# Seven products with four sums per side in the output projection and the feed-forward, the first normalisation on ScalarE

## The chip, the cores and the metric

The kernel runs on one core of a Trainium2 chip. The metric is the device time of one execution in microseconds (us). Times of several runs are given as their median; beside them stands one execution that the hardware profiler recorded, whose trace the profile is drawn from. The engines are TensorE (PE; its weight loads are listed apart as PEld), VectorE (DVE), ScalarE (ACT), GpSimd (POOL) and SyncE (SP), which here issues the DMAs.

## The reference, cut to what matters

One layer of a decoder block, 512 positions by 1024 channels, in float32:

```
p   = x @ W_in + b_in                       # split into u, v, q, k, v', r, low-rank gate, g_A, g_B
y_A = spatial gating unit(u, v)             # 128-position chunks, 8 groups
y_B = gated linear attention(q, k, v', ...) # 4 heads, RMSNorm, times silu(r)
m   = sigmoid(g_A) * y_A + sigmoid(g_B) * y_B
h   = LayerNorm(alpha * x + m @ W_out)              # W_out 1024 x 1024
out = LayerNorm(alpha * h + relu(h @ W_1)^2 @ W_2)  # W_1 1024 x 4096, W_2 4096 x 1024
```

The change touches the last two lines: the output projection with the first normalisation, and the feed-forward.

## The kernel before, in words

**Precision.** Each matmul operand is split (line 89 on ScalarE, line 90 on VectorE) into a high part, a cast to a shorter float format (fp32r), and a low part, the rest. A product is three matmuls: high by high, high by low, low by high.

**Weights.** All weights come in chunks of 128 x 1024 numbers, in the order that `_stream` lists. `load_to` issues the DMAs into a small ring, `sum_to` (line 124) forms sums or differences of chunks on VectorE where a product needs them, `split_to` splits a chunk into the next of seven pairs of buffers (wh, wl). A split therefore waits until TensorE has done with the chunk seven places back. Matmuls, and from line 588 on the instructions of VectorE, ScalarE and GpSimd too, run in the order in which the code emits them; DMAs on SP are placed by the compiler.

**Stages.** After the input projection, the gating unit and the attention (which are interleaved through slots, `at` and `pump`), `branch` handles two channel blocks of 128 at a time: two jobs for r, two for the gate B, each of 24 matmuls, and adds the result into AT_ (a view of bufA, channels on partitions). Each finished block is split into mh, ml, the operand of the output projection.

**Output projection.** Two calls of `row_unit` (columns 0 to 511, then 512 to 1023), each over four blocks of 128 rows, with 24 matmuls of 512 columns per block (line 213): 192 matmuls. `out_take` adds alpha * x on VectorE (line 869), takes statistics (870), and in the second call `ln_apply` normalises with scale g1 and shift b1 along the rows: two passes of 1024 on VectorE (640, 646), the power for 1/sqrt on GpSimd (171) between them.

**Turning.** The feed-forward needs h with channels on partitions. `turn_h` transposes a block of rows on TensorE (851) in two halves into the two PSUM banks of ps_a and splits each into hh, hl, which are the buffers of xh, xl. Rows 0 and 1 are turned during the second `row_unit`, rows 2 and 3 behind the first and third group of the feed-forward's first block: that block is run in two parts, positions 0 to 255, then 256 to 511.

**Feed-forward.** `col_group` (691) makes a hidden block of 128 channels in 24 matmuls; relu and square follow on ScalarE (915, 916). The second product, W_2, is done for three quarters of the hidden channels in pairs of blocks by seven block products instead of eight (`seven_products`, 986): operands are sums of blocks (`operand`, 912), each result is added to one of seven accumulators in SBUF (`keep`, 959 to 963), and `together` (997, 999) combines these at the end. One product alternates with one hidden block. The last quarter of W_2 is done plainly, row block by row block (1077), in column pieces of 512 and 512, for the last row block 512, 384 and 128; behind each piece VectorE adds and takes statistics (1078, 1079), and then normalises and stores the rows.

PSUM has eight banks: four single ones (ps_m), one pair (ps_s), and two single ones (ps_a).

Of the kernel before, what the change touches and what calls it, by code (L numbers as in the profile page):

```python
# [36 lines left out]
LANES = {0: RAW_BUFS, 1: 2}  # L37
PAIRS = 3
ORDER = (2, 6, 3, 7, 4, 1, 5)
LEVELS = (32, 8, 2)  # L40
ALS_AT = (0, 4, 48, 24, 12, 40, 56, 2)
# [5 lines left out]
def hybrid_block(  # L47
# [13 lines left out]
    ln1_b: bass.AP,  # L61
    ln2_g: bass.AP,
# [35 lines left out]
    raws, chunks, kept = {}, {}, {}  # L98
    lanes, ring = {0: rpool}, {lane: [] for lane in LANES}
    state = {"load": 0, "sum": 0, "split": 0}  # L100

    def load_to(n):
        while state["load"] < min(n, NCHUNK):
            i = state["load"]
            kind, lane, key, news = STREAM[i]
            if news is not None:
                ends = ring[lane]
                if len(ends) >= LANES[lane] and ends[-LANES[lane]] >= state["split"]:
                    break
                raw = lanes[lane].tile([P, 1024], F32, name=f"raw{i}", tag="raw")  # L110
                nc.sync.dma_start(raw, w_all[news])
                kept.setdefault(key, []).append(raw)
                users = [j for j in range(i + 1, NCHUNK) if STREAM[j][2] == key]
                users = [j for n_, j in enumerate(users) if all(STREAM[x][3] is None for x in users[:n_])]
                ends.append(max([i] + (users if key else [])))
            raws[i] = kept[key][-1:] if kind == "one" else kept[key][-2:]
            state["load"] = i + 1

    def sum_to(n):
        while state["sum"] < min(n, state["load"]):  # L120
            i = state["sum"]
            raw, *other = raws[i]
            if other:
                nc.vector.tensor_tensor(raw, raw, other[0], op=ALU.add if STREAM[i][0] == "sum" else ALU.subtract)  # L124
            state["sum"] = i + 1

    def split_to(n):
        n += n > ASIDE
        while state["split"] < min(n, NCHUNK):
# [8 lines left out]
            raw = raws[i][0]  # L138
# [4 lines left out]
        load_to(n + sum(LANES.values()) if 1 in lanes else n + RAW_BUFS)  # L143
# [106 lines left out]
    for i in range(4):  # L250
        raws[i] = [None]
# [31 lines left out]
    als_ = gt.tile([P, 1536], F32R, name="als", tag="qt", bufs=QT_BUFS)  # L283
    nc.vector.memset(als_.bitcast(F32), 0.0)
    als = []
    for k, o in enumerate(ALS_AT):
        als.append(als_[:, 192 * k + o : 192 * k + o + P])
        a4 = als[k].rearrange("p (r m) -> p r m", r=4)
        split(a4[:, 0, 0:RANK], a4[:, 3, 0:RANK], wal[:, k, :])
        nc.scalar.copy(a4[:, 1:3, 0:RANK], a4[:, 0:1, 0:RANK].bitcast(F32).broadcast_to([P, 2, RANK]))  # L290
# [32 lines left out]
    def low_rank():  # L323
        pa = ps_a.tile([P, 512], F32, name="pa", tag="aux")
        for k in range(KT):
            for i, xx in enumerate((xh, xl)):
                nc.tensor.matmul(
                    pa, als[k], xx[:, k, :], start=(k == 0 and i == 0), stop=(k == KT - 1 and i == 1)
# [465 lines left out]

    def r_take(e, t1):
# [25 lines left out]
    def branch(e0):  # L821
        t1 = {e: temp(f"t1_{e}", "brow") for e in (e0, e0 + 1)}
        for e in t1:
            col_job(f"r{e}", r_take(e, t1[e]))
        for e in t1:
            col_job(f"gb{e}", gb_take(e, t1[e]))
            if e0:
                split(mh[:, e, :], ml[:, e, :], AT_[:, e, :])

    branch(0)  # L830
# [6 lines left out]
    lnp.tile([P, 32], F32, name="pad_n")  # L837
    first_ln = ExitStack()
    ln1p = pool(first_ln, "ln1p", side="right")
    g1 = row_bcast(ln1p, ln1_g, D, "g1")  # L840
    b1 = row_bcast(ln1p, ln1_b, D, "b1")
    mstack = ExitStack()
    mpool = pool(mstack, "mpool", side="left")
    mh = mpool.tile([P, KT, T], F32R, name="mh")
    ml = mpool.tile([P, KT, T], F32R, name="ml")

    def turn(src, t, half, dh, dl):

        pt = ps_a.tile([P, 4, P], F32, name="pturn", tag="aux")
# [46 lines left out]

# [322 lines left out]
```

## Time and profile before

| | before |
|---|---|
| runs shown: median (lowest to highest) of 3 | 758.2 us (758.01 to 758.51) |
| the profiled execution | 757.96 us, span 756.2 us |
| granted TensorE clock, mean | 0.997 |

The page gives per engine the busy time, its share of the span and the instructions, then the span in 40 slices. The chain that ended last is followed back from the last instruction, and its shares say which engine the time hangs on. Groups of instructions by line show count, mean duration and what ended the idle time before them. A row of the timeline has start, duration, engine, line, operation, output and inputs, shapes, and a count where like instructions stand together. A row of the windows has for each stretch its length, the busy time of PE, PEld, DVE, ACT and POOL with the instructions in brackets, the granted clock, and the DMAs' share and rate. Matmuls are pipelined, so what one costs is read from start to start, not from its duration.

### The profile page before, as it was taken

How to read it: one execution, taken by the hardware profiler on the slowest of the kernel's cores; microseconds unless marked ns; L12 is line 12 of the kernel's file. 1: busy time of each engine (PE TensorE's matmuls, PEld its weight loads, DVE VectorE, ACT ScalarE, POOL GpSimd, SP SyncE). 2: the span in 40 equal slices, each digit the busy share in tenths (PEclk: the TensorE clock that was granted, in tenths of full speed). 3: DMA queues.
4: the chain of work that ended last, by engine and by line, in shares of the span. 5: the costliest groups of instructions: out<-in, count | busy, mean ns of one | idle time of the engine just before them, and what ended most of it. 6: DMA issues, size and time to landing. Idle time of an engine off the chain costs nothing.

```text
span 756.2 us, 8829 instructions
## 1 busy us (share of the span) xinstructions
PE 747.2 (99%) x3498; PEld 626.8 (83%) x3498; DVE 492.8 (65%) x618; ACT 349.5 (46%) x472; POOL 29.8 (4%) x60
## 2 busy tenths in 40 slices
PE   9999999999999999999999999999999999999996
PEld 7878888888888888888888988888888888888885
DVE  8478876676575554435458544874677667777995
ACT  7475744363254735444222544454644444445300
POOL 1000000000000102000002000000000000000011
PEclk9999999999999999999999999999999999999998
DMA  8623422222142131432341423444234333534111
GB/s 341 208 73 125 137 77 80 84 84 84 36 141 75 56 126 56 144 107 84 98 158 33 171 62 107 139 140 140 86 137 141 137 112 112 164 114 166 58 56 55
DMA packets 25465, 85.15 MB, mean 113 GB/s; under 512 B 3088, under 2 KB 3344, under 8 KB 25424
## 3 DMA queue, kind: packets, MB, share of 16 engines
q1 hardware_dynamic: 25280, 84.33, 32.4%
q8 instruction: 27, 0.44, 0.2%
q10 hardware_dynamic: 144, 0.26, 0.1%
q14 instruction: 14, 0.11, 0.1%
HBM read 82.48 MB, written 2.10 MB: 112 GB/s over the span
## 4 chain that ended last, share of the span: by engine, by line
PE 96%; issue 1%; DVE 1%; DMA 0%; POOL 0%; DVEq 0%; POOLq 0%
PE f L691 22%; PE ps L213 17%; PE m L986 15%; PE f L1077 6%; PE gb L691 6%; PE r L691 6%; PE ga L691 6%; PE u L691 6%; PE qk L691 3%; PE first L272 3%; PE sc L519 2%; PE pm L744 1%; PE po L553 1%; PE po L557 1%; PE po L555 1%
## 5 line engine op out<-in xcount | busy, mean ns | idle before, releaser
L90 DVE TENSOR_TENSOR wl<-raw,wh 128x1024 fp32r<-128x1024 f32 x141 | 171.2, 1222 | 99.2 <-ACT wh L89 97.7
L89 ACT CAST wh<-raw 128x1024 fp32r<-128x1024 f32 x141 | 145.7, 1044 | 51.1 <-PE ps L213 23.7
L691 PE MATMUL f<-xh,wh 128*128 128x512 f32 (+1 forms) x288 | 105.4, 366 | 0.0
L691 PE MATMUL f<-xl,wh 128*128 128x512 f32 (+1 forms) x288 | 105.3, 365 | 0.0
L691 PE MATMUL f<-xh,wl 128*128 128x512 f32 (+1 forms) x288 | 105.2, 365 | 0.0
L986 PE MATMUL m<-wh,oh 128*128 128x512 f32 x168 | 65.4, 389 | 0.0
L986 PE MATMUL m<-wl,oh 128*128 128x512 f32 x168 | 65.4, 389 | 0.0
L986 PE MATMUL m<-wh,ol 128*128 128x512 f32 x168 | 65.4, 389 | 0.0
L691 PEld LDWEIGHTS f<-xh,wl 128*128 128x128 f32 x288 | 54.3, 189 | 8.8
L691 PEld LDWEIGHTS f<-xh,wh 128*128 128x128 f32 x288 | 54.3, 189 | 8.7
L691 PEld LDWEIGHTS f<-xl,wh 128*128 128x128 f32 x288 | 54.3, 189 | 8.6
L213 PE MATMUL ps<-wh,xh 128*128 128x512 f32 x128 | 50.4, 394 | 0.0
L213 PE MATMUL ps<-wh,xl 128*128 128x512 f32 x128 | 49.8, 389 | 0.0
L213 PE MATMUL ps<-wl,xh 128*128 128x512 f32 x128 | 49.8, 389 | 0.0
L915 ACT ACTIVATE F<-f 128x512 f32<-128x512 f32 (+1 forms) x28 | 15.0, 536 | 70.7 <-PE f L691 70.7
L124 DVE TENSOR_TENSOR raw<-raw,raw 128x1024 f32<-128x1024 f32 x30 | 36.6, 1221 | 9.1 <-DMA raw<-in_w_all 9.1
L986 PEld LDWEIGHTS m<-wh,ol 128*128 128x128 f32 x168 | 31.5, 188 | 6.6
L986 PEld LDWEIGHTS m<-wh,oh 128*128 128x128 f32 x168 | 31.5, 188 | 6.6
L986 PEld LDWEIGHTS m<-wl,oh 128*128 128x128 f32 x168 | 31.5, 188 | 6.5
L89 ACT CAST oh<-d 128x1024 fp32r<-128x1024 f32 x15 | 15.7, 1049 | 36.4 <-DVE d L912 36.4
L90 DVE TENSOR_TENSOR ol<-d,oh 128x1024 fp32r<-128x1024 f32 x15 | 18.4, 1225 | 16.7 <-ACT oh L89 16.7
L213 PEld LDWEIGHTS ps<-wh,xl 128*128 128x128 f32 x128 | 24.0, 188 | 5.1
(231 smaller groups left out, 1477.1 us busy)
## 6 DMA issues: line engine op xcount, KB each, us to landing
raw<-in_w_all SPq DMA_DIRECT2D x136, 512.0 KB, 3.3
bufB<-in_head SPq DMA_DIRECT2D x4, 512.0 KB, 7.9
xr<-in_x SPq DMA_DIRECT2D x8, 256.0 KB, 3.6
out<-bufA SPq DMA_DIRECT2D x8, 256.0 KB, 2.0
bufA<-in_head SPq DMA_DIRECT2D x3, 512.0 KB, 5.3
brow<-in_b_in SPq DMA_DIRECT2D x4, 256.0 KB, 6.4
g<-in_ln_g SPq DMA_DIRECT2D x2, 512.0 KB, 4.0
b<-in_ln_b SPq DMA_DIRECT2D x2, 512.0 KB, 4.9
```

Source lines behind the costliest of these rows:

```text
L89: nc.scalar.copy(hi, src)
L90: nc.vector.tensor_tensor(lo, src, hi.bitcast(F32), op=ALU.subtract)
L124: nc.vector.tensor_tensor(raw, raw, other[0], op=ALU.add if STREAM[i][0] == "sum" else ALU.subtract)
L213: nc.tensor.matmul(ps, s_, m_, start=(k == 0 and i == 0), stop=(k == KT - 1 and i == 2))
L272: nc.tensor.matmul(first[e], s_, m_[:, k, :], start=(k == 0 and i == 0), stop=(k == KT - 1 and i == 2))
L519: nc.tensor.matmul(sc[:, c, 0:192], pr.kt[:, jc * P : (jc + 1) * P], pr.qt[:, jc, :], start=True, stop=True)
L553: nc.tensor.matmul(po, pr.AT[:, j, c, :], vs, start=True, stop=(c == 0))
L555: nc.tensor.matmul(po, pr.QI[:, j, c * P : (c + 1) * P], pr.S[j], start=False, stop=True)
L691: nc.tensor.matmul(ps, s_, m_, start=(k == 0 and i == 0), stop=(k == KT - 1 and i == 2))
L915: nc.scalar.activation(dst, ps, AF.Relu)
L986: nc.tensor.matmul(ps, s_, m_, start=(k == 0 and i == 0), stop=(k == 3 and i == 2))
L1077: nc.tensor.matmul(ps, s_, m_, start=(f == 0 and i == 0), stop=(f == 7 and i == 2))
```

## The change

The seven block products are done by another scheme, with a sum or difference in only four of seven operands on each side, and now in the output projection too. With A the left operand (positions by channels) and B the weights in 2 x 2 blocks:

```
product 1: A11 B11        2: A12 B21            5: S1 T1   S1 = A21+A22, T1 = B12-B11
product 6: S2 T2  S2 = S1-A11, T2 = B22-T1      3: S4 B22  S4 = A12-S2
product 7: S3 T3  S3 = A11-A21, T3 = B22-B12    4: A22 T4  T4 = B21-T2
x = 1, then +6, +7, +4 in one pair of PSUM banks (ps_s); v = 5, then +3 in ps_a
C11 = x(1) + 2;  C12 = x(1,6) + v(5,3);  C22 = v(5) + x(1,6,7);  C21 = x(1,6,7,4)
```

The order is 1, 2, 5, 6, 3, 7, 4. VectorE reads each bank after the product and adds it into bufA (projection) or bufB (feed-forward). The separate accumulators, the copies and `together` go. Products 7 and 4 follow each other on the same pair of banks; in the feed-forward a hidden block stands between any two products, in the projection none. The sums of the weights stay in SBUF (tiles "held", tags A and B), the ring of loads has three buffers, and W_out is laid out in quarters like W_2; two of its quarters are loaded twice.

The operands of the projection (seven blocks of 4 x 256 instead of the plain 8 x 512) are formed behind the branch jobs, whose channel blocks are paired anew. The first normalisation becomes one activation per row block on ScalarE without scale and shift; these are applied to channels in PSUM when the rows are turned, four pieces on ScalarE, four on VectorE, and for the kept rows by a multiplication and an addition on VectorE behind the jobs of the second hidden block. Rows 2 and 3 are turned behind the first and second group of the feed-forward. The operand of the low-rank gate is formed in fewer, larger instructions, in a buffer of the weights' ring. The last row block has pieces of 512, 256 and 256.

```diff
-ORDER = (2, 6, 3, 7, 4, 1, 5)
+ORDER = (1, 2, 5, 6, 3, 7, 4)
+PAIRED = ((0, 1), (4, 5), (2, 6), (3, 7))
...
+    def product_of(name, m, ops, take):
+        hi, lo = ops
+        u0 = take_chunks(2)
+        banks, begins = accumulators(m, name)
+        for t, ps in enumerate(banks):
+            tsl = slice(t * P, (t + 1) * P)
+            for k in range(4):
...
+                    nc.tensor.matmul(
+                        ps,
+                        s_,
+                        m_,
+                        start=(begins and k == 0 and i == 0),
...
+                if t and k % 2:
+                    split_to(u0 + k // 2 + 1 + W_BUFS)
+            take(m, t, ps)
...
+    def as_it_is(k, m, n=1):
...
+        split(mh[:, MADE[m] : MADE[m] + n, k, :], ml[:, MADE[m] : MADE[m] + n, k, :], src)
+
+    def summed(k):
...
+        nc.vector.tensor_tensor(s1, a(2, 1), a(2, 2), op=ALU.add)
+        for o, x_, y_ in ((s2, s1, a(1, 1)), (s4, a(1, 2), s2), (s3, a(1, 1), a(2, 1))):
+            nc.vector.tensor_tensor(o, x_, y_, op=ALU.subtract)
+        for i in range(2):
+            split(mh[:, 2 * i : 2 * i + 2, k, :], ml[:, 2 * i : 2 * i + 2, k, :], d[i])
...
+    branch(PAIRED[3], {3: [lambda: as_it_is(3, 1)], 7: [lambda: as_it_is(3, 2), *all_of(3)[1:]]})
...
+    def normalise(t):
+        row = bufA[:, t, :]
+        nc.scalar.activation(row, row, AF.Identity, bias=rs1[t][:, 1:2], scale=rs1[t][:, 0:1])
 
     def turn_h(t):
+
         for half in range(2):
-            turn(bufA[:, t, :], t, half, hh, hl)
-
-    row_unit(mh, ml, out_take(0))
-    at(S_O + 5, lambda: turn_h(0))
-    at(S_O + 6, lambda: turn_h(1))
-    row_unit(mh, ml, out_take(1))
+            pt = ps_a.tile([P, 4, P], F32, name="pturn", tag="aux")
+            for i in range(4):
+                e = half * 4 + i
+                nc.tensor.transpose(pt[:, i, :], bufA[:, t, e * P : (e + 1) * P], ident)
+            for i in range(4):
+                e = half * 4 + i
+                g_, b_ = ln1c[:, e : e + 1], ln1c[:, 8 + e : 9 + e]
+                if half:
+                    nc.vector.tensor_scalar(pt[:, i, :], pt[:, i, :], g_, b_, op0=ALU.mult, op1=ALU.add)
+                else:
+                    nc.scalar.activation(pt[:, i, :], pt[:, i, :], AF.Identity, bias=b_, scale=g_)
+            ks, tsl = slice(half * 4, half * 4 + 4), slice(t * P, (t + 1) * P)
+            split(hh[:, ks, tsl], hl[:, ks, tsl], pt)
+
+    def project_take(m, t, ps):
+        i, j = GOES[m]
+        dst, tt = quarter(bufA, i, j)[:, t, :], 2 * i + t
+        if m in NEW:
...
+            nc.vector.scalar_tensor_tensor(dst, xr, ALPHA, ps, op0=ALU.mult, op1=ALU.add)
+        else:
+            nc.vector.tensor_add(dst, dst, ps)
+        if m in (2, 3, 7, 4):
+            stats(tt, j)
+        if m in (3, 4):
+            rest_of_stats(tt)
+        if m == 7:
+            normalise(t)
+            if t:
+                turn_h(0)
+        if m == 4 and t == 0:
+            turn_h(1)
+        if m == 4 and t == 1:
+            normalise(2)
+
+    for m in ORDER:
+        product_of(f"o{m}", m, (mh[:, MADE[m]], ml[:, MADE[m]]), project_take)
+    normalise(3)
...
-            elif e in (0, 2):
-                turn_h(2 + e // 2)
-    for job in block(take_raw(F, 1)):
+            elif e in (0, 1):
+                turn_h(2 + e)
...
+    for t, job in enumerate(block(take_raw(F, 1))):
         job()
+        nc.vector.tensor_mul(bufA[:, t, :], bufA[:, t, :], g1)
+        nc.vector.tensor_add(bufA[:, t, :], bufA[:, t, :], b1)
...
-        pieces = ((0, 512), (512, 512)) if t < NT - 1 else ((0, 512), (512, 384), (896, 128))
+        pieces = ((0, 512), (512, 512)) if t < NT - 1 else ((0, 512), (512, 256), (768, 256))
```

More of the change, by code (lines that the diff above doesn't have):

```diff
@@ L104, in load_to @@
             i = state["load"]
[L105 to L108, printed above, removed]
+            c, own, *_ = STREAM[i]
+            if c is not None and own is None:
+                if len(ring) >= RAW_BUFS and ring[-RAW_BUFS] >= state["split"]:
                     break
[L110 to L116, printed above, removed]
+                kept[i] = rpool.tile([P, 1024], F32, name=f"raw{i}", tag="raw")
+                ring.append(i)
+            elif c is not None:
+                if "pool" not in held or held_to.get(own, -1) >= state["split"]:
+                    break
+                kept[i] = held[own] = held["pool"].tile([P, 1024], F32, name=f"raw{i}", tag=own)
+                held_to[own] = max(j for j in range(i, min(i + 40, NCHUNK)) if STREAM[j][3] == STREAM[i][3] and own in STREAM[j][2:])
+            if c is not None:
+                nc.sync.dma_start(kept[i], w_all[c])
             state["load"] = i + 1
@@ L121, in sum_to @@
             i = state["sum"]
-            raw, *other = raws[i]
-            if other:
-                nc.vector.tensor_tensor(raw, raw, other[0], op=ALU.add if STREAM[i][0] == "sum" else ALU.subtract)
+            _, own, dst, _, less = STREAM[i]
+            if dst is not None:
+                raw = held[dst]
+                if less:
+                    x_, y_ = (held[a] if a else kept[i] for a in less)
+                    nc.vector.tensor_tensor(raw, x_, y_, op=ALU.subtract)
+                kept[i] = raw
             state["sum"] = i + 1
@@ L843, in hybrid_block @@
     mpool = pool(mstack, "mpool", side="left")
[L844 to L849, printed above, removed]
-        for i in range(4):
-            nc.tensor.transpose(pt[:, i, :], src[:, (half * 4 + i) * P : (half * 4 + i + 1) * P], ident)
-        ks, tsl = slice(half * 4, half * 4 + 4), slice(t * P, (t + 1) * P)
-        split(dh[:, ks, tsl], dl[:, ks, tsl], pt)
@@ L855, in hybrid_block @@
[L855 to L876 removed]
+    mh = mpool.tile([P, 7, 4, 256], F32R, name="mh")
@@ L1079, in hybrid_block @@
             nc.vector.bn_stats(st2[t][:, pi, :], z[:, sl])
-            for part in later.get((t, pi), ()):
-                together(*part)
         mv = lnp.tile([P, 2], F32, name=f"mv_l2{t}", tag="mv", bufs=4)
@@ L1118, in _stream @@
     n = 15 * 4
-    out = [("one", 0, None, None)] * 4 + [("one", 0, None, c) for c in range(n)]
+    out = [(None, None, None, None, None)] * 4 + [(c, None, None, None, None) for c in range(n - 8)]
     f1 = n
@@ L1142, in _stream @@
             out += take(1 + (i == 0)) + product
-    out += [("one", 0, None, f2 + 8 * PAIRS + c) for c in range(8 * (DF // 1024 - PAIRS))]
+    out += [(f2 + 8 * PAIRS + c, None, None, None, None) for c in range(8 * (DF // 1024 - PAIRS))]
     return out
```

235 lines of the change are left out of this document (105 added, 130 removed).

## The prediction

> **What bounds the kernel now.** I read the page first: the share of each engine, then the chain that ended last.
>
> ```profile
> span 756.2 us, 8829 instructions
> ...
> PE 747.2 (99%) x3498; PEld 626.8 (83%) x3498; DVE 492.8 (65%) x618; ACT 349.5 (46%) x472; POOL 29.8 (4%) x60
> ...
> PE 96%; issue 1%; DVE 1%; DMA 0%; POOL 0%; DVEq 0%; POOLq 0%
> ```
>
> TensorE is the chain. To see what one matmul is worth I took the chain in order of time, where matmuls of one kind stand merged, and the windows view for the output projection.
>
> ```profile
> 367.46 32.64 PE ps L213 x144
> ...
> 423.57 47.06 PE f L691 x264
> 470.64 5.44 PE m L986 x24
> ```
>
> ```profile
> 367.46:412.60 45.14, 45.14 (x209) 37.53 (x208) 28.68 (x39) 11.78 (x14) 4.56 (x3) 1.00 0.28 92
> ```
>
> 24 matmuls of 512 columns advance the clock by 5.44 us, 0.2267 us each, although the groups show about 0.39 us for one: they overlap. The window begins at 367.46, where the last branch job (gb7) ends; I count from there below ("at 0"). PE is busy in all 45.14 us, VectorE in 28.68. So what PE issues less is gained in full, as long as VectorE, which has 16 us to spare there, can take what the change gives it.
>
> The third view is PE's timeline at the seam to the feed-forward, the only place there where PE waits.
>
> ```profile
> 412.61 0.28 PE L691 MATMUL f<-xh,wh 128*128 128x256 f32 x1
> ...
> 415.48 1.04 PE L851 MATMUL pturn<-ident,bufA 128*128 128x128 f32 x8
> 416.27 0.36 PE L691 MATMUL f<-xh,wh 128*128 128x256 f32 x1
> ...
> 421.99 0.28 PE L691 MATMUL f<-xh,wl 128*128 128x256 f32 x1
> 422.32 1.25 PE L851 MATMUL pturn<-ident,bufA 128*128 128x128 f32 x8
> 423.33 0.36 PE L691 MATMUL f<-xh,wh 128*128 128x256 f32 x1
> ```
>
> Here 24 matmuls of 256 columns take 415.48 - 412.61 = 2.87 us (0.12 each) and the eight transposes of one row block 0.79 us. Before 422.32 PE waits 0.2 us, and the second four transposes wait again: the row block before them still holds the two PSUM banks of ps_a. That small wait is the one to watch.
>
> **The change, part by part.** *Fewer matmuls.* The projection has 7 x 24 = 168 matmuls for 192: 24 x 0.2267 = 5.44 us less on PE. The feed-forward had seven products before; PE does the same there.
>
> *The tail.* These are the second and third piece of the last rows and the add behind them.
>
> ```profile
> 742.52 0.33 PE L1077 MATMUL f<-wh,Fs 128*128 128x384 f32 x1
> ...
> 746.71 0.22 PE L1077 MATMUL f<-wh,Fs 128*128 128x128 f32 x1
> ...
> 749.22 0.28 PE L1077 MATMUL f<-wh,xl 128*128 128x128 f32 x1
> 749.53 0.29 DVE L1078 TENSOR_TENSOR bufB<-bufB,f 128x128 f32<-128x128 f32 x1 [1.48 <-PE f L1077]
> ```
>
> From 742.52 to the last add are 7.01 us. Two pieces of 256 take 48 x 0.12 = 5.76 us, with the 0.31 - 0.12 us behind the last start 5.95: 1.06 us less. The last add and statistics are 128 columns wider, 2 x 0.13 us back. Net -0.8 us.
>
> *VectorE in the projection.* Durations of the operations that the new order strings together:
>
> ```profile
> L124 DVE TENSOR_TENSOR raw<-raw,raw 128x1024 f32<-128x1024 f32 x30 | 36.6, 1221 | 9.1 <-DMA raw<-in_w_all 9.1
> ```
>
> ```profile
> 92.77 2.16 DVE L726 SCALAR_TENSOR_TENSOR mixb<-pb,cols_sb,mixb 128x128 f32<-128x128 f32 x8
> ...
> 368.22 0.69 DVE L816 TENSOR_TENSOR gb<-gb,t 128x512 f32<-128x512 f32 x1 [2.28 <-ACT gb L815]
> ...
> 411.17 1.28 DVE L90 TENSOR_TENSOR xl<-pturn,xh 128x512 fp32r<-128x512 f32 x2
> 412.37 3.49 DVE L90 TENSOR_TENSOR wl<-raw,wh 128x1024 fp32r<-128x1024 f32 x3
> 415.77 0.68 DVE L869 SCALAR_TENSOR_TENSOR bufA<-xr,ps 128x512 f32<-128x512 f32 x1
> 416.48 0.69 DVE L870 BATCH_NORM_STATS2 st<-bufA 128x6 f32<-128x512 f32 x1
> 417.21 0.21 DVE L638 BATCH_NORM_AGGREGATE mv_l<-st 128x2 f32<-128x12 f32 x1
> ...
> 417.53 1.28 DVE L640 SCALAR_TENSOR_TENSOR bufA<-bufA,mv_l,g 128x1024 f32<-128x1024 f32 x1
> ```
>
> From start to start a 1024-wide operation occupies VectorE for (3.49 - 1.22)/2 = 1.14 us, a 512-wide one 0.61, by their slope a 256-wide one 0.34, a 128-wide one 0.26. A result taken from PSUM with statistics is 0.71 + 0.61 = 1.32, with the end of the statistics 417.53 - 415.77 = 1.76. VectorE, ScalarE and GpSimd run in the order of the code from line 588 on, so I can keep an account.
>
> A weight chunk now serves 12 matmuls (2.72 us), not 24, so a split comes twice as often; and each product set needs eight weight sums. At 0.76 VectorE starts the end of gb7 (mul and add 1.3). Then sum and split of a chunk 2.3, and the last channels' four sums and four splits 4 x 0.34 + 2 x 0.34 + 2 x 0.61, about 3.6 with hand-overs: it is free at 8.0. Products 1, 2, 5, 6, 3, 7 each bring two splits (2.28) and two results; sums fall in 2 and 5 (two each, 2.28):
>
> product 1: 2.28 + 2 x 0.61 = 3.5, to 11.5; product 2: 4.56 + 2 x 1.32 = 7.2, to 18.7; product 5: 4.56 + 1.22 = 5.8, to 24.5; product 6: 3.5, to 28.0; product 3: 2.28 + 2 x 1.76 = 5.8, to 33.8; product 7: 2.28 + 2.64 = 4.9, to 38.7.
>
> PE is through these six products at 6 x 5.44 = 32.6. VectorE is 6 us behind when the turning of the rows begins. Up to there PE loses only about 1 us (products 3 and 4 wait for a bank to be read out).
>
> *The turning.* turn_h now scales and shifts in PSUM before it splits: half 0 by four ScalarE operations of 128 columns, half 1 by four on VectorE (4 x 0.26 = 1.04). Its price on ScalarE and the rest of the chain come from these rows.
>
> ```profile
> 400.58 1.07 ACT L89 CAST xh<-pturn 128x512 fp32r<-128x512 f32 x2 [8.50 <-PE pturn L851]
> ```
>
> ```profile
> 422.30 0.38 ACT L915 ACTIVATE F<-f 128x256 f32<-128x256 f32 x1 [1.95 <-PE f L691]
> 422.72 0.42 ACT L916 ACTIVATE F<-F 128x256 f32<-128x256 f32 x1
> 423.04 1.16 ACT L89 CAST xh<-pturn 128x512 fp32r<-128x512 f32 x2
> ```
>
> ```profile
> L673 ACT ACTIVATE bufB<-bufB,rs_sg 128x1024 f32<-128x1024 f32 x4 | 4.9, 1233 | 0.0
> ```
>
> ```profile
> L171 POOL TENSOR_TENSOR rs_l<-rs_l,nhalf 128x1 f32<-128x1 f32 x4 | 6.1, 1520 | 111.8 <-DVE rs_l L168 111.8
> ...
> L171 POOL TENSOR_TENSOR rs_sg<-rs_sg,nhalf 128x1 f32<-128x1 f32 x4 | 2.2, 551 | 63.9 <-DVE rs_sg L168 63.9
> L654 POOL TENSOR_SCALAR rs_sg<-mv_sg,rs_sg 128x1 f32<-128x1 f32 x4 | 1.1, 264 | 0.4
> ```
>
> No row shows a 128-wide activation with two column operands from PSUM to PSUM. It lies between VectorE's 0.26 and the 0.49 of a 512-wide cast; I take 0.36, near the middle. normalise is the 1.23 of L673; the power on GpSimd is 0.55 to 1.52 (1.52 where VectorE starts a 1024-wide operation at once); I take 0.55 for the last row block, behind which VectorE has nothing to do.
>
> Rows 0: VectorE subtracts half 0 (0.61, to 39.3), scales half 1 (1.04, to 40.4), waits 0.7 for ScalarE's cast and subtracts half 1, to 41.7. Only then are both banks free, so PE, which ended product 4's first half at 37.2, gets rows 1 turned at 42.1 and runs the second half to 44.8: about 4.1 us of waiting. Feed-forward group e0 follows, to about 47.8; rows 2 wait 1 us for their normalisation.
>
> Meanwhile VectorE: results of product 4, first half 1.76 (43.4), rows 1 as before 3.0 (46.4), two splits 2.6 (49.0), second half 1.76 (50.8); GpSimd 0.15 + 0.55 + 0.26 (51.8); ScalarE normalise(3) 1.23 (53.0). normalise(3) stands ahead of e0's relu and square in ScalarE's order, and these (0.74, to 53.7) ahead of the scaling of rows 2 (1.44, then cast 0.6, to 55.8). VectorE subtracts (56.5), scales, and ends half 1 at 58.9. Rows 3, turned behind e1 now and not e2, need these banks: PE, free since 53, waits till 59 with 0.4 us of transposes between: 6 us. Groups e2 and e3 end at 59.4 + 5.74 = 65.1.
>
> In the profile of before e3 ends at 423.33 + 2.87 = 426.2, 58.7 after gb7. So this stretch grows by 6.4 us, where its matmuls and transposes alone (38.1 + 3.2 + 11.5 = 52.8) would make it 5.9 shorter.
>
> *At nothing.* The scale and shift of the kept rows (8 x 1.14 us on VectorE) lie beside the next four jobs, 21.8 us of PE. The sums left out behind the products (L997, L999), the accumulators and the copies (L961) lay beside PE, which never waited for them. In the feed-forward 7 and 4, which share banks, have a job between them, so VectorE may be 8 us late. The low-rank operand is ready in fewer operations than before, ahead of the matmuls that use it. Four more loads of 0.5 MB and the smaller ring stay under splits that come every 2.7 us; if a load is late there, VectorE's account moves by that.
>
> **Sum.** The profiled execution took 757.96 us (its span and 1.8 us around it), the median of the runs is 758.2. 757.96 + 6.4 - 0.8 = 763.6 us. Bounds: operations on VectorE 5% cheaper with 0.26 for ScalarE's and 0.2 for its own 128-wide: 3 us less, 760.5; 5% dearer, with 0.45: 2.5 more, 766.1.
>
> **Rivals.** *VectorE keeps pace.* It is at 65% over the span and had 16 us to spare in this window; if the strung operations take some 15% less than these spacings, or the banks come free as PE needs them, nothing is late: 757.96 - 5.9 - 0.8 = 751.2, faster. Against it: the spacings are those of the same operations in a full queue, the account has no gap, and the wait for normalise(3) is one of order, not of load.
>
> *The clock falls in the waits.* This row is the first work of PE.
>
> ```profile
> 1.07 3.81 PE L248 MATMUL wu<-ones 128*128 128x128 f32 x18 [1.07 <-POOL bal L294]
> ```
>
> It shows 0.21 us for one, against 0.10 for the transposes above, the same shape and type: PE begins at half speed. If a wait of 4 us brings that back, some 3.8 us run at half speed behind it, 1.9 us more: 765.5, twice that if both long waits do it. No row of before can tell, since PE never waits that long there. The Trainium skill's page "TensorE: Matmul & The Clock Gate", section Part 1, states that an idle window of about 3.4 us halves the clock until about 3.4 us of work have passed; by it the two waits are just around the limit, and the estimate would be 1.7 us for each that trips it, 765.3 us for one.
>
> *Half the waits.* If rows 3 find their banks in time, because rows 2 are drained early, and only the waits in product 4 stay, the 6 us are not lost: 763.6 - 6 = 757.6, no change. For it: PE had only 0.2 us to wait there before. Against it: normalise(3).
>
> **How the numbers follow.** Forecast 0.60; the clock 0.17; half the waits 0.05; VectorE keeps pace 0.18. The likeliest gives 763.6. The range reaches from half the waits to the clock's upper case: 757.0 to 768.5, and leaves out the fast rival and little else. A difference under 0.2% (1.5 us) can't be told from none: faster 0.18, same 0.05, slower 0.77.
>
> **What would show it.** In the profile after: VectorE without gaps from gb7 to the end of product 4; PE waiting 2 us twice inside product 4 and about 4 and 2 us around the turning of rows 3, each ended by VectorE's split of pturn; no waits later; 168 matmuls at 0.227 us. It is wrong if PE runs through the seam, if the waits sit in the feed-forward products, or if matmuls behind the waits are slow.

## The result and the profile after

The changed kernel takes 837.34 us (median; 837.0 to 839.4) beside 758.11 us for the kernel before on the same chip: ratio 1.105, 95% interval 1.1031 to 1.1069. The direction was forecast, the size was not: 79.2 us more and not 5.4. The page of the changed kernel, again the shares, the chain and TensorE's clock:

```profile
span 835.5 us, 8843 instructions
...
PE 766.1 (92%) x3474; PEld 635.7 (76%) x3474; DVE 510.2 (61%) x653; ACT 366.0 (44%) x484; POOL 27.9 (3%) x64
...
PEclk9999999999999999998997999899998999989999
...
PE 83%; DVE 9%; ACT 5%; issue 2%; POOL 0%; DVEq 0%; ACTq 0%; POOLq 0%
```

TensorE has 24 matmuls fewer, and yet 18.9 us more busy time; it is idle for 69.4 us where it was idle for 9.0. VectorE is on the chain with 9%. So there are waits, and matmuls have become slower. To see where, I cut both kernels at the same matmuls (the first of the projection, the first with 512 columns of the second hidden block, the first of the tail) and took the windows view of the pieces. I call the first piece the seam stretch (projection, turning, first hidden block) and the second the feed-forward. Columns: the window, its length, busy time of PE, PEld, DVE, ACT and POOL, TensorE's granted clock, share of the DMA engines, GB/s. First the changed kernel:

```profile
367.22:463.47 96.25, 75.10 (x394) 64.59 (x393) 59.77 (x89) 42.23 (x65) 4.14 (x8) 0.88 0.37 128
463.47:784.21 320.74, 281.68 (x1178) 228.15 (x1177) 189.39 (x186) 129.95 (x158) 0.00 (x0) 0.95 0.30 99
784.21:835.50 51.29, 44.02 (x217) 37.24 (x215) 25.78 (x45) 1.05 (x1) 3.95 (x4) 0.96 0.11 42
```

Then the kernel before:

```profile
367.30:437.81 70.51, 70.45 (x418) 62.45 (x416) 43.02 (x55) 23.07 (x36) 6.08 (x4) 1.00 0.35 119
437.81:704.39 266.58, 266.58 (x1178) 220.73 (x1177) 182.32 (x175) 133.22 (x168) 0.00 (x0) 1.00 0.37 125
704.39:756.20 51.81, 45.11 (x217) 38.28 (x215) 40.12 (x67) 2.00 (x3) 3.94 (x4) 0.96 0.13 49
```

The seam stretch grew by 25.7 us, the feed-forward by 54.2, the tail shrank by 0.5. In the feed-forward both kernels have the same 1178 matmuls; the changed one has 39.1 us without any, and 15.1 us more of busy time at a clock of 0.95. PE's waits, with total, number and longest:

```profile
PE mx L832 <- DVE bufB L1036: 29.0, 9, 4.9
PE mx L832 <- DVE bufB L1034: 10.0, 3, 4.9
PE mxo L832 <- DVE bufA L959: 9.1, 2, 6.1
PE pturn L942 <- DVE xl L90: 7.8, 3, 4.0
PE mxo L832 <- DVE bufA L961: 4.2, 2, 2.2
```

16 of the waits are of one kind: a matmul into mx waits for VectorE to have read mx out (L959 and L961 are the readouts in the projection, L1034 and L1036 in the feed-forward). There are four such products (1, 6, 7, 4) in each of four sets, so each waits once. The timeline around one shows where (start, duration):

```profile
594.02 0.39 PE L832 MATMUL mx<-wh,oh 128*128 128x512 f32 x1
...
596.45 1.23 DVE L90 TENSOR_TENSOR wl<-raw,wh 128x1024 fp32r<-128x1024 f32 x1 [3.08 <-ACT wh L89]
596.51 0.39 PE L832 MATMUL mx<-wh,ol 128*128 128x512 f32 x1
597.59 1.22 DVE L90 TENSOR_TENSOR ol<-F,oh 128x1024 fp32r<-128x1024 f32 x1
598.73 0.68 DVE L1036 TENSOR_TENSOR bufB<-bufB,mx 128x512 f32<-128x512 f32 x1
599.46 0.80 PE L832 MATMUL mx<-wh,oh 128*128 128x512 f32 x1 [2.56 <-DVE bufB L1036]
600.05 0.63 PE L832 MATMUL mx<-wl,oh 128*128 128x512 f32 x1
600.48 0.63 PE L832 MATMUL mx<-wh,ol 128*128 128x512 f32 x1
...
602.62 0.43 PE L832 MATMUL mx<-wl,oh 128*128 128x512 f32 x1
602.88 0.39 PE L832 MATMUL mx<-wh,ol 128*128 128x512 f32 x1
```

The twelve matmuls from 594.02 to 596.51 make the first half (t = 0) of a product. The second half writes another PSUM bank, and still starts only when VectorE has read out the first. Both banks are slices of one tile (`x_ = ps_s.tile([P, 2, 512], ...)`, line 814), and the wait is set for the tile. VectorE has the split of a weight chunk and that of the next operand to do first, because these stand ahead of the readout in the code: 2.56 us. Then the second thing: behind the wait the matmuls follow one another at 0.43 us, not 0.2267, for some 2.6 us. TensorE runs at half speed.

**Theory.** The tile of two banks makes the second half of each product that adds to x wait for the readout of the first; the longer of these waits bring the half clock. **Rivals.** VectorE is late all along and the tile only shows it. Or adding in PSUM (start=False) is slow by itself. What is left without the waits should be my forecast.

### The profile page after: what moved, and what is told of

Same layout as the page of the kernel before. It is cut to its first block, busy times and chain, and to the rows that moved or that the text cites. A ratio compares the mean times of both kernels' runs of the same rounds, so it can differ in the third digit from the quotient of the medians.

```text
span 835.5 us, 8843 instructions
## 1 busy us (share of the span) xinstructions
PE 766.1 (92%) x3474; PEld 635.7 (76%) x3474; DVE 510.2 (61%) x653; ACT 366.0 (44%) x484; POOL 27.9 (3%) x64
## 4 chain that ended last, share of the span: by engine, by line
PE 83%; DVE 9%; ACT 5%; issue 2%; POOL 0%; DVEq 0%; ACTq 0%; POOLq 0%
PE f L692 21%; PE ps L219 10%; PE mx L832 6%; PE f L1121 5%; PE gb L692 5%; PE r L692 5%; PE ga L692 5%; PE u L692 5%; PE mv L832 4%; DVE wl L90 3%; PE first L276 3%; PE qk L692 3%; ACT wh L89 2%; PE m L832 2%; PE sc L520 2%
## 5 line engine op out<-in xcount | busy, mean ns | idle before, releaser
L90 DVE TENSOR_TENSOR wl<-raw,wh 128x1024 fp32r<-128x1024 f32 x147 | 178.7, 1223 | 168.4 <-ACT wh L89 167.1
L89 ACT CAST wh<-raw 128x1024 fp32r<-128x1024 f32 x147 | 152.1, 1044 | 102.6 <-PE mx L832 59.3
L832 PE MATMUL mx<-wh,oh 128*128 128x512 f32 x96 | 43.8, 456 | 39.1 <-DVE bufB L1036 29.0
L832 PEld LDWEIGHTS mx<-wh,oh 128*128 128x128 f32 x96 | 20.8, 217 | 48.4 <-DVE bufB L1036 32.8
L832 PE MATMUL mx<-wl,oh 128*128 128x512 f32 x96 | 41.9, 437 | 0.0
L832 PE MATMUL mx<-wh,ol 128*128 128x512 f32 x96 | 41.4, 431 | 0.0
L219 PEld LDWEIGHTS ps<-wl,xh 128*128 128x128 f32 x128 | 24.0, 188 | 4.9
L219 PEld LDWEIGHTS ps<-wh,xh 128*128 128x128 f32 x128 | 24.0, 188 | 4.8
L832 PE MATMUL mxo<-wh,mh 128*128 128x512 f32 x32 | 15.3, 479 | 13.3 <-DVE bufA L959 9.1
L692 PE MATMUL u<-xh,wh 128*128 128x512 f32 x64 | 25.9, 405 | 0.0
```

Source lines behind the costliest of these rows:

```text
L89: nc.scalar.copy(hi, src)
L90: nc.vector.tensor_tensor(lo, src, hi.bitcast(F32), op=ALU.subtract)
L219: nc.tensor.matmul(ps, s_, m_, start=(k == 0 and i == 0), stop=(k == KT - 1 and i == 2))
L692: nc.tensor.matmul(ps, s_, m_, start=(k == 0 and i == 0), stop=(k == KT - 1 and i == 2))
L832: nc.tensor.matmul(ps, s_, m_, start=(begins and k == 0 and i == 0), stop=(k == 3 and i == 2), skip_group_check=True,)
```

## The experiments: the tile

**Two tiles.** The one suspected cause away: ps_s is closed behind the last branch job, and the two banks become two tiles.

```diff
-                x_ = ps_s.tile([P, 2, 512], F32, name=f"mx{name}", tag="sc")
-                sums["x"] = [x_[:, t, :] for t in range(2)]
+                sums["x"] = [ps_x.tile([P, 512], F32, name=f"mx{name}_{t}", tag=f"x{t}") for t in range(2)]
```

> The changed kernel with one edit: the two banks of the sum that products 1, 6, 7 and 4 share are two tiles of one bank each, not one tile of two. Theory (the second half of each such product waits until VectorE has read out the first half, because both lie in one tile; 16 such waits, 12 of them in the feed-forward, and slow matmuls behind each): all 16 waits go, the clock stays full in the feed-forward, and what is left is the seam as forecast, about 763.6 us (759 to 768), the feed-forward from e2 to the tail within 2 us of the 284.1 us of before. Rival 1 (VectorE is late all along, the tile only shows it): the waits stay at the first half of the next product, over 810 us. Rival 2 (adding in PSUM is itself slower on TensorE): waits go but matmuls stay slow, about 837.3 - 52.3 = 785 us.

770.72 us, ratio 1.0166 (1.015 to 1.0181): 66.6 us of the 79.2 are gone. The windows of this kernel, the six products up to the turning, the turning and product 4, the first hidden block, and the feed-forward:

```profile
367.43:400.36 32.93, 32.71 (x144) 26.77 (x143) 32.38 (x43) 14.26 (x17) 2.23 (x2) 1.00 0.53 177
400.36:418.93 18.57, 11.49 (x42) 8.62 (x41) 13.92 (x26) 10.44 (x17) 1.63 (x4) 0.72 0.36 125
418.93:451.72 32.79, 27.30 (x209) 26.69 (x208) 12.91 (x21) 17.12 (x32) 0.82 (x2) 0.90 0.37 127
451.72:718.31 266.59, 266.59 (x1179) 220.80 (x1177) 185.67 (x183) 128.46 (x158) 0.00 (x0) 1.00 0.35 117
```

The feed-forward takes 266.59 us, as before the change (266.58), with no gap and the clock at 1.00. VectorE does the same work there as in the changed kernel, and PSUM sums are added as there: both rivals fall. What is left is the seam stretch, 84.29 us where it was 70.51. The kernel is 7.1 us above my forecast, and the section on the seam is about that.

**Two tiles in the feed-forward only.** The projection keeps its tile of two banks:

```diff
+                if name[0] == "o":
+                    x_ = ps_s.tile([P, 2, 512], F32, name=f"mx{name}", tag="sc")
+                    sums["x"] = [x_[:, t, :] for t in range(2)]
+                else:
+                    sums["x"] = [ps_x.tile([P, 512], F32, name=f"mx{name}_{t}", tag=f"x{t}") for t in range(2)]
```

> The changed kernel with two tiles in the feed-forward only; the projection keeps the tile of two banks. Theory: the 56.1 us that the feed-forward grew by go, 781 us (777 to 785), and the stretch from gb7 to e3 stays at 82.4 us. Rival 1: over 810 us, as the waits come back elsewhere. Rival 2 (adding in PSUM is slow by itself): about 837.3 minus 12 waits of 3 to 4 us each, 790 to 800 us.

783.56 us (ratio 1.0334, 1.0316 to 1.0352), with the feed-forward at 266.59 us and the seam stretch at 97.3. So of the 66.6 us, 53.8 are the feed-forward's and 12.8 the projection's.

**The tile alone, in the kernel before.** Nothing of the change is in it but this:

```diff
+            if m in (1, 6, 7, 4):
+                mx = ps_s.tile([P, 2, 512], F32, name=f"mx{p}_{m}", tag="sc")
             for t in range(2):
                 tsl = slice(t * P, (t + 1) * P)
-                ps = ps_m.tile([P, 512], F32, name=f"m{p}_{m}_{t}", tag="ps")
+                if m in (1, 6, 7, 4):
+                    ps = mx[:, t, :]
+                else:
+                    ps = ps_m.tile([P, 512], F32, name=f"m{p}_{m}_{t}", tag="ps")
```

> The kernel before with the one suspected cause added: its products 1, 6, 7 and 4 of the feed-forward write both halves of their result into one tile of two banks, where each half had a tile of its own. Nothing is added up in PSUM, and the projection stays as it was. Theory (the tile alone makes the second half wait for VectorE's readout of the first): 12 waits in the feed-forward as in the changed kernel, 35 to 56 us slower than before, 793 to 814 us. Rival (the waits need the sums in PSUM or the changed kernel's heavier load on VectorE as well): under 10 us slower, 758 to 768 us.

819.92 us (ratio 1.0822, 1.0791 to 1.0852): 61.8 us more, over the upper end of what I expected, from an edit that changes no arithmetic and adds no instruction. Its waits and its feed-forward:

```profile
PE mx L991 <- DVE bufB L963: 21.1, 6, 4.9
PE mx L991 <- DVE acc L963: 9.8, 2, 4.9
...
PE mx L991 <- ACT acc L961: 3.5, 1, 3.5
```

```profile
437.80:767.50 329.70, 286.65 (x1178) 231.85 (x1177) 183.56 (x176) 134.31 (x168) 0.00 (x0) 0.94 0.31 102
```

There are twelve waits, one for each of these products, and each stands at the first matmul of the second half. 43 us without a matmul and 20 us more busy time at a clock of 0.94: the picture of the changed kernel, in a kernel that has neither its sums nor its order.

**The clock.** The changed kernel with its tile of two banks, and nine more matmuls, whose result nobody uses, ahead of each waiting half:

```diff
+    def keep_warm(name, hi, wh, n=9):
+        spare = ps_m.tile([P, 512], F32, name=f"warm{name}", tag="ps")
+        for i in range(n):
+            nc.tensor.matmul(spare, hi[:, 0, 0:P], wh[:, 0:512], start=True, stop=True)
...
+            if t and m in (1, 6, 7, 4):
+                keep_warm(name, hi, chunks[u0][0])
```

> The changed kernel, with the tile of two banks, and nine matmuls of 512 columns more (2.04 us) into a spare PSUM bank, whose result nobody uses, ahead of the second half of each of the 28 products' 16 that share banks. Theory of the clock (a wait of 2 to 6 us halves the clock for some 3 us behind it): the extra matmuls lie in waits of at least 2.1 us, so they cost nothing and leave too little idle time for the clock to fall: the slow matmuls go, 16 x 1.4 = 22 us less, about 815 us. Rival (the matmuls are slow for another reason, for example their source or the sum in PSUM): no gain, 837 us or up to 16 x 2.04 = 33 us more, 870 us.

830.09 us (ratio 1.0946, 1.0928 to 1.0965): 7.3 us less with 33 us of matmuls more, not the 22 less that I expected. The timeline at the place shown above:

```profile
594.53 2.20 PE L826 MATMUL warm<-wh,oh 128*128 128x512 f32 x9
597.26 0.50 PE L839 MATMUL mx<-wh,oh 128*128 128x512 f32 x1 [0.52 <-DVE bufB L1043]
597.59 0.39 PE L839 MATMUL mx<-wl,oh 128*128 128x512 f32 x1
597.82 0.40 PE L839 MATMUL mx<-wh,ol 128*128 128x512 f32 x1
```

0.52 us of the wait is left, and the matmuls behind it are at full speed. So idle time is what halves the clock. My 22 us were too many for two reasons. Not every wait does it: in the changed kernel's feed-forward 51 matmuls ran slow (over 0.6 us each) behind 6 of the 12 waits, 51 x 0.2 = 10.2 us; the other 4.9 of the 15.1 us lie at the twelve restarts, in which the last matmul ahead of the wait and the first behind it overlap with nothing (about 0.3 us at full clock, 0.5 us where the first one is slow). And waits of 4.9 us became 2.9, which still halved the clock: 27 slow matmuls are left, so 24 x 0.2 = 4.8 us were gained, of the 5.4 us by which the feed-forward is shorter (315.35).

## The experiments: the seam

With two tiles the seam stretch is what I had forecast to grow by 6.4 us, and it grew by 13.8. PE's turning of rows 1 in that kernel, then ScalarE and VectorE ahead of it:

```profile
409.87 1.11 PE L945 MATMUL pturn<-ident,bufA 128*128 128x128 f32 x4 [4.71 <-DVE xl L91]
412.90 1.11 PE L945 MATMUL pturn<-ident,bufA 128*128 128x128 f32 x4 [1.92 <-DVE xl L91]
413.67 0.78 PE L832 MATMUL mxo<-wh,mh 128*128 128x512 f32 x1
414.24 0.63 PE L832 MATMUL mxo<-wl,mh 128*128 128x512 f32 x1
414.67 0.63 PE L832 MATMUL mxo<-wh,ml 128*128 128x512 f32 x1
```

```profile
404.57 1.05 ACT L90 CAST wh<-raw 128x1024 fp32r<-128x1024 f32 x1 [2.48 <-DMA raw<-in_w_all]
405.52 1.24 ACT L937 ACTIVATE bufA<-bufA,rs_l 128x1024 f32<-128x1024 f32 x1
406.67 1.80 ACT L952 ACTIVATE pturn<-pturn,ln1c 128x128 f32<-128x128 f32 x4
```

```profile
405.65 1.23 DVE L91 TENSOR_TENSOR wl<-raw,wh 128x1024 fp32r<-128x1024 f32 x1 [1.70 <-ACT wh L90]
...
409.12 0.69 DVE L91 TENSOR_TENSOR xl<-pturn,xh 128x512 fp32r<-128x512 f32 x1 [0.92 <-ACT xh L90]
409.73 1.78 DVE L950 TENSOR_SCALAR pturn<-pturn,ln1c 128x128 f32<-128x128 f32 x4
```

Three things are to be seen: the second bank comes 3.03 us behind the first; all of product 4's second half then runs at 0.43 us; and ScalarE, ahead of all this, stands 2.48 us at a cast whose weights have not landed, with the normalisation of rows 1 and the scaling of rows 0 behind it in the order of the code, and VectorE waits 1.70 us for that cast.

**The seam's order.** normalise(3) behind the first group's relu, square and the scaling of rows 2; rows 3 turned behind e2.

```diff
-    normalise(3)
...
-            elif e in (0, 1):
-                turn_h(2 + e)
+            elif e in (0, 2):
+                turn_h(2 + e // 2)
+                if e == 0:
+                    normalise(3)
```

> The kernel with two tiles throughout, and at the seam two steps moved: normalise(3) stands behind the first group's relu and square and the scaling of rows 2, and rows 3 are turned behind e2, not e1. If the forecast's seam is right (waits of 4 and 2 us there, from order and not from load), it is 3 to 6 us faster than the kernel with two tiles alone, 758 to 760 us. Rival (VectorE is late by load at the seam, 6 us behind whatever the order): within 1 us of the kernel with two tiles alone, as rows 3 wait later for the same splits.

765.51 us (ratio 1.0096, 1.0081 to 1.0111): 5.2 us less than with two tiles alone. The waits at rows 3 (3.57 and 1.92 us) are gone; those at rows 1 stay (3.81 and 1.91). So at rows 3 it was the order. The following kernels build on this one.

**Banks, work and chain.** Four edits, alone and together: rows 1 and 3 turned in banks of ps_m; the sums of weights left out; the sums on GpSimd; the scale and shift left out.

```diff
-            pt = ps_a.tile([P, 4, P], F32, name="pturn", tag="aux")
+            pt = (ps_m if t % 2 else ps_a).tile([P, 4, P], F32, name="pturn", tag="ps" if t % 2 else "aux")
```

```diff
-        return (c, own, dst, p, less)
+        return (c, own, dst, p, less if p >= 0 else None)
```

```diff
-                    nc.vector.tensor_tensor(raw, x_, y_, op=ALU.subtract)
+                    engine = nc.gpsimd if i < 70 else nc.vector
+                    engine.tensor_tensor(raw, x_, y_, op=ALU.subtract)
```

```diff
-            for i in range(4):
-                e = half * 4 + i
...
-                    nc.scalar.activation(pt[:, i, :], pt[:, i, :], AF.Identity, bias=b_, scale=g_)
```

> The kernel with two tiles and the moved seam; rows 1 and 3 are turned in two banks of the pool ps_m, rows 0 and 2 in ps_a as before, so that no row block waits for the banks of the one before it. Theory of the banks: the waits of 3.8 and 1.9 us at rows 1 go, and the slow matmuls behind them: about 8 us less than the 765.5 us of the kernel with the moved seam, 757 to 758. Theory of the load (VectorE is about 6 us behind by then, whoever holds the banks): the wait moves to the first group of the feed-forward, which needs rows 1 split; 0 to 4 us less, 761.5 to 765.5.

> The kernel with two tiles and the moved seam, without the eight sums of weights of the projection (so its seven products take plain quarters of the weights; the output isn't the reference's): 8 x 1.14 = 9.1 us less work for VectorE there. Theory of the load: the waits at rows 1 shrink from 5.7 to under 2.5 us and bring no slow matmuls, 759 to 761 us. Theory of the banks: rows 0 hold both banks for as long as their chain of scale, cast and difference takes, whatever the load; within 1.5 us of 765.5.

> The kernel with two tiles and the moved seam, the eight sums of weights of the projection on GpSimd, not VectorE. By the theory of the load, if GpSimd takes less than the 5.4 us of a product for two of them and does not slow VectorE, the same gain as without the sums, 759 to 761 us. Rival (GpSimd is slow, or slows VectorE beside it): splits come late for products 5, 6, 7 and 4, and TensorE waits there for weights; 770 us or more.

> The kernel with two tiles and the moved seam, with both: rows 1 and 3 turned in banks of ps_m, and the eight sums of weights of the projection left out (the output isn't the reference's). Alone, the first gained 0.3 us and the second 3.8. Theory (load and banks are two limits in a row, each hiding the other): both together gain more than their sum, 758.5 to 760.5 us. Rival (what is left at the seam is the length of the chain of one row block, normalise, turn, scale, split, behind product 7): 761 to 762 us, with the wait at the first group of the feed-forward.

> The kernel with two tiles and the moved seam, the scale and shift of the first normalisation left out in the turning (4 x 0.45 us of ScalarE and 4 x 0.44 us of VectorE for each row block; the feed-forward then gets rows that are normalised alone, and the output isn't the reference's). Theory (VectorE's load and the length of the chain set the wait at rows 1): both lose 1.8 us for a row block, the wait of 3.8 and 1.9 us shrinks by 3 to 4 us and brings no or few slow matmuls: 760 to 762 us. Rival (VectorE is behind by its work ahead of the turning, not in it): less than 2 us gained, over 763.5 us.

> All three: four banks, no sums of weights in the projection, no scale and shift (the last two make another output than the reference's). If banks, load and chain are all that stands between this and the forecast's fast rival, no wait over 0.5 us is left at the seam and it takes 751 to 754 us. Rival (something that none of the three touches, such as GpSimd's power or the normalisation on ScalarE, holds the rows): 756 us or more.

| kernel | median us | seam stretch us | from, to |
|---|---|---|---|
| before | 757.9 to 758.2 | 70.51 | 367.30, 437.81 |
| two tiles | 770.72 | 84.29 | 367.43, 451.72 |
| two tiles, seam's order | 765.51 | 77.60 | 367.25, 444.85 |
| the same and four banks | 765.26 | 78.00 | 367.68, 445.68 |
| the same and no sums | 761.73 | 74.12 | 367.15, 441.27 |
| the same and sums on GpSimd | 766.08 | 78.93 | 367.08, 446.01 |
| the same and four banks, no sums | 761.37 | 73.83 | 366.96, 440.79 |
| the same and no scale and shift | 758.78 | 71.26 | 367.78, 439.04 |
| the same and four banks, no sums, no scale and shift | 751.68 | 64.85 | 367.60, 432.45 |

("The same" is the kernel with two tiles and the seam's order. The feed-forward takes 266.6 us in all of them.) Four banks gain nothing: the wait moves, as the theory of the load had it, to the first group, which needs rows 1 split:

```profile
PE f L693 <- ACT xh L90: 4.6, 2, 3.9
```

Banks and sums together gain no more than the sums alone, so these two don't hide each other. GpSimd takes 2.4 to 3.0 us for a sum, and nothing is gained: ScalarE waits up to 3.56 us for such a sum, VectorE ends the statistics of product 3 only 0.2 us earlier, and the wait for the load stays (2.63 us). The scale and shift alone are worth 6.7 us, more than I expected of them. All three together leave no wait:

```profile
367.60:432.45 64.85, 64.85 (x393) 57.94 (x392) 46.04 (x66) 35.23 (x49) 4.13 (x8) 1.00 0.47 158
```

The stretch is then 5.7 us shorter than before the change, and the kernel takes 751.68 us (ratio 0.9916, 0.99 to 0.9933): the fast rival of the forecast, 751.2, at the price of leaving out a part.

**The late load.** Without the sums ScalarE does not wait for a load there. To take the load apart from VectorE's work, the last split of product 7 was put behind the results of that product and the turning of rows 0, with the sums where they were; once more with four banks, and once with four banks and the sums on GpSimd.

```diff
+                late = name == "o7" and k == 3
-                if t and k % 2:
+                if t and k % 2 and not late:
                     split_to(u0 + k // 2 + 1 + W_BUFS)
             take(m, t, ps)
+            if t and late:
+                split_to(u0 + 2 + W_BUFS)
```

> The kernel with two tiles and the moved seam (765.5 us); the last split of product 7, whose weights land 1.6 to 2.5 us late, stands behind the results of product 7, the normalisation of rows 1 and the turning of rows 0, not ahead of them. Theory of the load: rows 0 leave their banks 1.5 to 3 us earlier, and it takes 762.5 to 764 us. Theory of VectorE's work alone (the wait for the load lies beside a backlog): within 1 us of 765.5.

> The same split moved, in the kernel with four banks for the turning (765.3 us). Theory of the load: the chain of rows 1, which sets the start of the feed-forward there, is 2 to 3 us earlier: 762 to 763.5 us. Theory of VectorE's work alone: within 1 us of 765.3.

> The split moved, four banks, and the eight sums of weights of the projection on GpSimd (2.4 to 3.0 us each there). Nothing is left out. If VectorE's work and the load are both limits, 759 to 761 us, the fastest of the kernels with seven products in the projection that compute all; if GpSimd delays the splits as it may have before (766.1 us with it), 764 us or more.

763.42, 763.58 and 764.06 us (ratios 1.0071, 1.0074, 1.008, each within 0.0014). So taking the late load out of the chain is worth 2.1 us. Leaving out the sums took it out too, so some 2 us of their 3.8 are probably the load's; no run separates the two. GpSimd adds nothing again. The fastest kernel with seven products in the projection that computes all is this 763.4 us, 5.4 us over the kernel before. What keeps it there, by the run without scale and shift, is above all the chain of a row block (normalise, turn, scale, cast, difference) with its four 128-wide operations of 0.45 us on either engine.

**The clock at the seam.** Extra matmuls again, here on the kernel with two tiles: 16 and 12 ahead of the turning of rows 1 and 3; then 18 and 13, with 8 more between the two halves of each (the diff shows the second).

```diff
         if m == 4 and t == 0:
+            warm(mh[:, MADE[4]].rearrange("p k t -> p (k t)"), 18)
             turn_h(1)
...
             elif e in (0, 1):
+                if e:
+                    warm(chunks[u0 + e][0], 13)
                 turn_h(2 + e)
...
         for half in range(2):
+            if half and t in (1, 3):
+                warm(chunks[unit["next"] - 1][0], 8)
```

> The kernel with two tiles alone (770.7 us), and 16 and 12 matmuls of 512 columns more (3.6 and 2.7 us, results not used) ahead of the turning of rows 1 and of rows 3, inside the waits of 4.7 and 3.6 us there. Theory of the clock: the extra matmuls cost nothing and the 11 matmuls of 512 and 12 of 256 columns that run at half speed behind the waits (about 3.7 us) run at full speed: 767 to 768 us. Rival (the slow matmuls come from the transposes or from writes beside them): 770 us or more.

> The kernel with two tiles, with 18 and 13 extra matmuls of 512 columns (4.1 and 2.9 us, results not used) ahead of the turning of rows 1 and rows 3, and 8 (1.8 us) between the two halves of each of these, where 1.9 to 2.4 us of waiting were left. Theory of the clock: no wait over 1 us is left there, no matmul behind runs at half speed, and it takes about 3.5 us less than the kernel with two tiles alone (770.7): 766.5 to 768. Rival (the slow matmuls are not from idle time, or the extra ones push the transposes back by as much as they gain): 770 us or more.

The first gave 770.42 us, no difference: a wait of 2.37 us was left behind the extra matmuls, and eight matmuls behind it still ran at 0.43. The second gave 768.94 us (ratio 1.0138, 1.0121 to 1.0155), 1.8 us less than with two tiles alone, about half of what I expected, and no slow matmul:

```profile
405.13 4.24 PE L961 MATMUL warm<-mh 128*128 128x512 f32 x18
409.87 0.66 PE L947 MATMUL pturn<-ident,bufA 128*128 128x128 f32 x4 [0.50 <-DVE xl L91]
410.29 2.09 PE L961 MATMUL warm<-wh 128*128 128x512 f32 x8
412.91 0.66 PE L947 MATMUL pturn<-ident,bufA 128*128 128x128 f32 x4 [0.53 <-DVE xl L91]
```

The transposes of rows 1 stand where they stood, at 409.87 and 412.9: this wait is VectorE's. What ran slow behind it is gained, and a part of that is given back, for the rows behind come hardly earlier (the last transposes of rows 3 start at 432.34, 64.9 behind the start, without the extra matmuls, and at 431.75, 64.2 behind it, with them; the forecast had 59). So of the 7.1 us between the kernel with two tiles and the forecast about 1.8 come back when the clock stays full; the rest stays, and goes with the late chain of the rows.

No kernel here that computes all beats the kernel before. The projection of before with the feed-forward of the change in two tiles wasn't tried: from the stretches (266.59 and 266.58, a tail 0.5 us shorter) it would differ by less than can be measured.

## Why the prediction was wrong

**The step that failed** is in the part headed "At nothing": "In the feed-forward 7 and 4, which share banks, have a job between them, so VectorE may be 8 us late." It counts from one product to the next, and by banks. The code has one tile for both banks of x, and the program waits for tiles: what counts is the distance from the first half's last matmul to the second half's first, which is nothing. So every microsecond in which VectorE is late there is TensorE's, and the readout stands behind two to five operations in VectorE's order. The price was 66.6 us (two tiles against one), and the same tile costs the kernel before 61.8. The Trainium skill's page "Perfetto Trace Analysis", section Matmuls, asks that independent matmul groups rotate through different PSUM banks so that reading one out overlaps the next group's matmuls. The halves did so, and yet waited up to 6.1 us; the trace agrees with the rule only once each bank is a tile of its own (266.59 us without a gap). The fact could be read before: line 814 was in the full diff, and the page of the changed kernel only showed it. Two of the signs of being wrong that the forecast named came with it: waits in the feed-forward's products, and slow matmuls behind the waits.

**What was right.** 24 matmuls less: the stretch without any wait is 64.85 us against 70.51, 5.7 less where the forecast had 5.9. The tail: 0.5 less, forecast 0.8. VectorE's account up to product 7: with two tiles VectorE takes up the first result 8.2 us behind the start (375.65 - 367.43), forecast 8.0, and the results of product 7 at 34.0 (401.42), forecast 33.8; it is busy for 32.38 of the 32.93 us of the six products, while TensorE loses only 0.2 there.

**The seam, mis-sized.** The forecast had rows 0 give back the first bank at 39.3 and the second at 41.7, and rows 1 turned at 42.1. With two tiles the banks came at 42.4 and 45.5 (409.87 and 412.90), and rows 1 were turned at 46.2 (413.67). Two terms were too small. The loads were put at nothing, with the remark that a late one would move VectorE's account; one was late, and VectorE waited 1.70 us for its split and 0.92 us for ScalarE behind it. And one 128-wide operation took 0.44 us on VectorE and 0.45 on ScalarE, not 0.26 and 0.36. (The 0.26 fits the row of eight such operations at 92.77; the slope that the forecast names gives 0.21.) Product 4's second half ended at 51.5 (418.93), not 44.8: 4.1 us by the banks, the rest by the half clock. Behind that the forecast's two waits at rows 3, 4 and 2 us, are there with 3.57 and 1.92. In the changed kernel itself these two are 4.00 and 1.92. By the windows the stretch has 84.29 - 71.50 = 12.8 us without a matmul, close to the forecast's 1 + 4.1 + 1 + 6 = 12.1. That is partly luck: the wait at rows 1 was 6.6 us for 4.1, the one at rows 3 5.5 for 6, and the two of 1 us came to 0.7. What the forecast lacked are the 71.50 - 64.85 = 6.65 us by which TensorE is busy longer, in slow matmuls and restarts. With the slow ones gone most of that came back as waiting, since the chain behind is late too.

**The rivals.** VectorE did not keep pace. The rival of the clock was right in kind: I gave it one or two places at the seam, and the changed kernel has ten stretches at half clock between the projection and the tail, six of them in the feed-forward. Half the waits: the waits at rows 3 were the half that an order could remove, as the moved seam showed, but not with a gain over before.

## What to carry to other kernels

Ask of every buffer what the program waits for: the tile, not the bank or the slice. Where two halves of a result share a tile, the second half waits for the first one's readout, and that readout for all that stands ahead of it on its engine. An engine at 65% that stands outside the chain costs nothing until a matmul waits for its next instruction; then its whole queue is on the chain. And price a wait of TensorE with what comes behind it: the restart, and the half clock, which here followed 5 of the 13 waits of some 2.6 us and all 14 from 2.9 us on.

## What the runs showed of the hardware

The clock falls in shorter waits than I had thought. Over the feed-forwards of the changed kernel, of the one with extra matmuls and of the kernel before with the tile: behind the waits of up to 1.80 us none of 9 brought slow matmuls, of those of 2.56 to 2.62 us 5 of 13 did, of those from 2.86 to 4.91 us all 14. The slow matmuls came at 0.427 us, for 2 to 5.5 us. The Trainium skill's page "TensorE: Matmul & The Clock Gate", Part 1, gives a start-to-start of 426.7 ns for 512 columns at the half clock, and the trace agrees.

What decides is where a wait falls. The traces record the granted clock, and in each of these three the stretches at half clock last 3.41 us or a multiple of it and begin on one grid of 3.41 us (the last one is cut off by the end). These are windows of that grid in the changed kernel, two around the wait of 2.56 us shown above, which brought the half clock, and three around the wait of 2.56 us that ends at 501.57, which did not:

```profile
595.83:599.24 3.41, 1.07 (x5) 0.56 (x3) 2.79 (x3) 1.53 (x2) 0.00 (x0) 1.00 0.24 88
599.24:602.65 3.41, 3.19 (x8) 2.51 (x9) 0.17 (x1) 0.22 (x1) 0.00 (x0) 0.50 0.00 0
...
496.84:500.25 3.41, 2.17 (x10) 1.47 (x8) 1.69 (x2) 2.60 (x4) 0.00 (x0) 1.00 0.76 287
500.25:503.67 3.42, 2.10 (x9) 1.73 (x10) 1.26 (x2) 0.39 (x1) 0.00 (x0) 1.00 0.02 5
503.67:507.08 3.41, 3.41 (x17) 2.81 (x16) 2.72 (x3) 1.72 (x2) 0.00 (x0) 1.00 0.01 2
```

The first wait leaves 2.34 us idle in one window, and the next window has the half clock; the second is cut in two by the grid, 1.24 and 1.32 us, and the clock stays. So it is for all 36 waits: behind the 19 that put 2.05 us or more into one window the clock fell, behind the 17 that put 1.76 us or less it did not. That all 14 of the longer waits were followed by it is thus a count and not a bound, for the grid can cut the shorter of them in two as well. The Trainium skill's same part has the half clock follow at least one idle window of about 3.4 us, free-running. The grid of 3.41 us agrees with that; that 2.05 us idle in a window was enough does not, and the measurement decides.

A 128-wide operation from PSUM to PSUM with two column operands took about three quarters of the time of a 512-wide cast: four took 1.78 us on VectorE and 1.80 us on ScalarE, beside 0.59 for ScalarE's cast of all 512 columns (with two tiles).
